# The first two projection blocks are begun without the adaLN shift, which is added later as a bias

## The chip, the cores and the metric

One core of one Trainium2 chip runs the whole program. The metric is device microseconds of one execution, on that core. TensorE is called PE here, the loads of its weights PEld, VectorE DVE, ScalarE ACT, GpSimd POOL, and SP is the queue engine that issues most DMAs.

## What is computed

One layer of a streaming encoder, for 1,024 prompt rows and 32 sample rows of width 1,024 (together 1,056 columns when transposed). Only the beginning matters here:

```python
mod = jax.nn.silu(c) @ w_ada + b_ada                # c: one row for the prompt, one for the sample
sh1, sc1, gt1, sh2, sc2, gt2 = jnp.split(mod[:, None, :], 6, axis=-1)
h = rmsnorm(x, g_mix) * (1 + sc1) + sh1
u = h @ w_in                                        # w_in: 1024 x 5640
qa, ka, va, qm, km, vm, om, ip, fp, ga, gm = jnp.split(u, _split_points(), axis=-1)
...
merged = (jax.nn.sigmoid(ga) * (ya @ w_br_att) + jax.nn.sigmoid(gm) * (ym @ w_br_mlstm))
x = x + gt1 * (merged @ w_out)
```

Band attention (`qa`, `ka`, `va`), an mLSTM (`qm` to `fp`), the merge by the gate columns `ga` and `gm`, and a SwiGLU FFN follow. Everything is float32, and a matmul of float32 precision is made from three passes over operands split in a high and a low part.

## The kernel before, in words

Activations stand transposed, 128 channels by 1,056 columns, in eight such rows of tiles (index `j` or `k`, 0 to 7). The 1,056 columns are taken in three tiles of 352, the constant `TILES`; the third tile holds the last 320 prompt columns and the 32 sample columns. `h` is kept as eight tiles `[128, 2, 1056]`, where part 0 is the value rounded to the matmul's type (written by ACT) and part 1 the remainder (written by DVE). A weight block is 128 columns of `w_in`, split the same way. One block times one tile is 8 x 3 = 24 matmuls of 128x352 (`unit`), a whole block 72.

Every engine runs its instructions in the order in which the program writes them (`manual_schedule`); DMAs on SP's queue also start in order, and each waits for the earlier DMA that used the same one of eight semaphores. The SBUF pool `slots` has 16 buffers of 128x2x1056, which hold in turn the rows of x, x transposed, the adaLN columns, normalised x and h; the pool `wsp` has four buffers for split weights; PSUM's pool `mm` has three buffers of 128x512.

The front runs like this:

- SP loads the small parameters, x, the adaLN weight's first 2,048 columns (`load_ada`, shift and scale together, eight loads of 128x2048), and weight blocks. PE transposes x (line 300), ACT copies it out of PSUM.
- `first_ada` makes shift and scale from these columns. PE takes ten of sixteen 128-column groups (line 337); DVE multiplies and adds six for both vectors of c (lines 341 and 343), and PE sums those over the partitions (line 351).
- `first_mod` adds the bias of adaLN and makes `sh1` and `s1` (lines 361, 364). `scaled_x` (line 373) makes x times scale and 1/rms, and `first_h` adds shift: ACT the high part (line 380), DVE the low part (line 384).
- x transposed is stored to DRAM as `xres` (eight stores, line 1438), for the residual sum much later.
- `first_units` (line 460) runs k_block(0) and v_block(0), the attention's first key and value blocks, together: per `k` three tiles of both blocks, as soon as h's tile `k` is there. Six PSUM tiles hold the sums.

Then `segs` lists segments of blocks. The first has k, v and q of the first two heads, the following ones the other blocks while attention and the mLSTM run beside them in steps that a counter releases (`side`). Sixteen blocks are gates; `gate_block` copies each tile out of PSUM and stores it to DRAM (`g_d`). Eight of the gate blocks stand in the last segment, beside the second half of the mLSTM.

Of the kernel before, what the change touches and what calls it, by code (L numbers as in the profile page):

```python
# [12 lines left out]
ALU = mybir.AluOpType  # L13
# [126 lines left out]
def hybrid_stream_step(  # L140
# [75 lines left out]
    sp.dma_start(prow[R_C:R_C + 8], c_prompt.rearrange("o (r c) -> (o r) c", c=P))  # L216
    sp.dma_start(prow[R_C + 8:R_C + 16], c_sample.rearrange("o (r c) -> (o r) c", c=P))
    xtok = []
    def param_loads():
        sp.dma_start(prow[R_ADA:R_ADA + 48], b_ada.rearrange("o (r c) -> (o r) c", c=P))  # L220
        sp.dma_start(prow[R_GMIX:R_GMIX + 8], g_mix.rearrange("o (r c) -> (o r) c", c=P))
        sp.dma_start(prow[R_GFFN:R_GFFN + 8], g_ffn.rearrange("o (r c) -> (o r) c", c=P))
        sp.dma_start(prow[R_GAIN:R_GAIN + 4], mh_gain.rearrange("o (r c) -> (o r) c", c=P))
        sp.dma_start(prow[R_CW:R_CW + 32], conv_w.rearrange("o j (r c) -> (o j r) c", c=P))
        sp.dma_start(prow[R_CB:R_CB + 8], conv_b.rearrange("o (r c) -> (o r) c", c=P))

    for i in range(KD):
        if i % 2 == 0:
            xt = slot([P, 2, D])
            xtok += [xt[:, 0], xt[:, 1]]  # L230
        sp.dma_start(xtok[i], xp[i * P:(i + 1) * P])
        if i == 3:
            param_loads()
# [47 lines left out]
    was = []  # L281

    def load_ada(n):
        while len(was) < n:
            wa = slot([P, 2048])
            sp.dma_start(wa, w_ada[len(was) * P:(len(was) + 1) * P, 0:2048])
            was.append(wa)

    load_ada(5)
# [34 lines left out]
    psA = [ps_s(), ps_t()]  # L324
    NV = 6
    acv = [tmpt((P, NV * P)) for _ in range(2)]

    def first_ada():
        load_ada(6)
        W.load(2)  # L330
        load_ada(KD)
        W.load(3)
        for k in range(KD):
            c = csil[:, k].unsqueeze(1).to_broadcast([P, DH, 2])
            for b in (*range(8, 16), *range(NV, 8)):
                out = psA[b // 8][:, (b % 8) * P:(b % 8 + 1) * P]
                pe.matmul(out.rearrange("p (r c) -> p r c", c=2), was[k][:, b * P:(b + 1) * P], c,
                          start=(k == 0 and b in (NV, 8, 12)), stop=(k == KD - 1), skip_group_check=True)
            for c in range(2):
                if k == 0:  # L340
                    dve.tensor_scalar(acv[c], was[k][:, :NV * P], csil[:, k, c:c + 1], None, op0=ALU.mult)
                else:
                    dve.scalar_tensor_tensor(acv[c], was[k][:, :NV * P], csil[:, k, c:c + 1], acv[c],
                                             op0=ALU.mult, op1=ALU.add)
            if k == 0:
                bcast_cols(RB, rstd, [P] * 8 + [TS], 0)
            if k == 3:
                W.advance()
        for b in range(NV):
            for c in range(2):  # L350
                pe.matmul(psA[0][:, b * P + c:b * P + c + 1], acv[c][:, b * P:(b + 1) * P], ones[:, 0:1],
                          start=(b + c == 0), stop=True, skip_group_check=True)
# [4 lines left out]
    def first_mod(i, a=0, b=KD):  # L357
        x = (sh1, s1)[i][:, :, a:b]
        p3 = psA[i].rearrange("p (b r) -> p r b", r=P)
        o = R_ADA + 8 * i  # L360
        dve.tensor_tensor(x, p3[:, 0:2, a:b], cols[:, o + a:o + b].unsqueeze(1).to_broadcast([P, 2, b - a]),
                          op=ALU.add)
        if i:
            dve.scalar_tensor_tensor(s1, s1, 1.0, bc2(cols[:, R_GMIX:R_GMIX + 8]), op0=ALU.add, op1=ALU.mult)

    hs = []

    def scaled_x(j):
# [3 lines left out]
        for c, a, b in col_segments(0, T):  # L372
            dve.scalar_tensor_tensor(xns[j][:, a:b], xTs[j][:, a:b], s1[:, c, j:j + 1], RB[:, a:b],
                                     op0=ALU.mult, op1=ALU.mult)

    def first_h(j):

        h = slot([P, 2, T], F32R)
        for c, a, b in col_segments(0, T):
            act.activation(h[:, 0, a:b], xns[j][:, a:b], AF.Identity, bias=sh1[:, c, j:j + 1])  # L380
        if j + 1 < KD:
            scaled_x(j + 1)
        for c, a, b in col_segments(0, T):
            dve.scalar_tensor_tensor(h[:, 1, a:b], xns[j][:, a:b], sh1[:, c, j:j + 1], f(h[:, 0, a:b]),
                                     op0=ALU.add, op1=ALU.subtract)
        hs.append(h)
# [10 lines left out]
    def weight(parts, nk, uses=3, home=None):  # L397
# [10 lines left out]
        def split(raw):  # L408
# [5 lines left out]
            for i, t in enumerate(wt):  # L414
                n = min(4, nk - 4 * i)
                split_to(t[:, :, :n], raw[:, 4 * i:4 * i + n], pool if (W.done or home is slots) and not hm_n[1] else dve)
# [21 lines left out]
    first = {}  # L438

    def first_units(ws):  # L440

        wts = [W.use(w) for w in ws]
        S, PT = ps_s(), ps_t()
        pts = [[mmt() for _ in TILES], [S[:, :512], S[:, 512:], PT[:, :512]]]
        for k in range(KD):
# [4 lines left out]
            if k == 6:  # L450
                W.advance()
# [1727 lines left out]
```

## Time and profile before

| | us |
|---|---|
| median of 3 runs (1636.94 to 1639.3) | 1638.59 |
| the profiled execution | 1638.16 |
| span of its profile | 1636.4 |
| PE busy | 1588.6 |
| DVE busy | 1123.2 |
| ACT busy | 782.3 |
| POOL busy | 535.7 |

The profile is one execution. In a row of a timeline the first two numbers are start and duration in us, xN is a count of instructions merged, and the bracket is the engine's idle time before the row with what ended it. In a group the numbers behind the bar are busy us, the mean in ns of one, and idle us before. A stretch A:B shows busy us of each engine, the share of full clock that PE was granted, the share of the DMA engines and GB/s. A name such as "s<-mm" says what is written and what is read.

### The profile page before, as it was taken

What the parts mean: (1) busy time and instruction counts of PE and PEld (TensorE: products, weight loads), DVE (VectorE), ACT (ScalarE), POOL (GpSimd) and SP (SyncE); (2) the same over time, 40 slices, a digit from 0 to 9 for tenths busy, and PEclk for the clock granted to TensorE, in tenths of its full rate; (3) what the DMA queues carried; (4) which work ended last, traced back from release to release, by engine and by line L of the source; (5) the groups of instructions that cost most, each with busy time, mean ns of one, the idle gap of its engine ahead of it and who ended that gap; (6) DMA issues with size and microseconds to landing.
All of it is one profiled execution on the core that took longest, in us unless ns stands there. A gap on an engine that the chain in (4) does not pass through costs nothing.

```text
span 1636.4 us, 27518 instructions
## 1 busy us (share of the span) xinstructions
PE 1588.6 (97%) x10324; PEld 1567.1 (96%) x10324; DVE 1123.2 (69%) x2100; ACT 782.3 (48%) x1735; POOL 535.7 (33%) x537
## 2 busy tenths in 40 slices
PE   6989999999999999999999998999999999999997
PEld 6989999999999999999999988999999999999997
DVE  6756564546776745446655688889888886898654
ACT  3455454543555544443434545454544444554443
POOL 1234333433432311000012146556565652233101
PEclk9999999999999999999999999999999999999999
DMA  9732323232232232574453311223223227426454
GB/s 338 249 107 75 106 81 106 68 120 79 76 94 79 59 100 69 118 275 160 129 151 107 98 53 40 92 66 103 80 67 103 66 82 246 132 78 236 133 158 126
DMA packets 210327, 192.45 MB, mean 118 GB/s; under 512 B 10571, under 2 KB 180531, under 8 KB 209171
## 3 DMA queue, kind: packets, MB, share of 16 engines
q1 hardware_dynamic: 205554, 187.88, 36.9%
q10 hardware_dynamic: 4640, 2.82, 0.6%
q8 instruction: 81, 1.33, 0.3%
q14 instruction: 52, 0.42, 0.1%
HBM read 152.19 MB, written 41.63 MB: 118 GB/s over the span
## 4 chain that ended last, share of the span: by engine, by line
PE 82%; DVE 6%; ACT 3%; issue 2%; DMA 1%; POOL 0%; ACTq 0%; POOLq 0%; DVEq 0%
PE mm L428 36%; PE psb L1727 27%; PE psb L2131 5%; PE psb L1974 3%; PE mm L826 2%; PE psV L725 2%; PE psS L667 1%; PE psT L694 1%; DVE s L1577 1%; DVE wsp L395 1%; DVE sl L1564 1%; DVE st L681 1%; PE psV L1060 1%; ACT st L682 1%; PE psT L1062 1%
## 5 line engine op out<-in xcount | busy, mean ns | idle before, releaser
L428 PE MATMUL mm<-s,wsp 128*128 128x352 f32 x4104 | 690.4, 324 | 5.7 <-DVE t L1658 1.9
L428 PEld LDWEIGHTS mm<-s,wsp 128*128 128x128 f32 x4104 | 656.8, 188 | 8.9 <-DVE stg L518 2.2
L1727 PE MATMUL psb<-s,wsp 128*128 128x352 f32 x2544 | 421.0, 323 | 8.9 <-DVE wsp L395 2.8
L1727 PEld LDWEIGHTS psb<-s,wsp 128*128 128x128 f32 x2544 | 411.1, 189 | 10.8 <-issue 5.3
L395 DVE TENSOR_TENSOR wsp<-wraw,wsp 128x512 fp32r<-128x512 f32 (+1 forms) x284 | 245.4, 882 | 126.0 <-ACT wsp L394 124.1
L394 ACT ACTIVATE wsp<-wraw 128x512 fp32r<-128x512 f32 x340 | 201.6, 617 | 144.9 <-PE psb L1727 81.9
L687 POOL TENSOR_SCALAR st<-st,mx 128x640 f32<-128x640 f32 (+5 forms) x72 | 55.6, 773 | 191.5 <-DVE mx L686 177.2
L1142 DVE SCALAR_TENSOR_TENSOR t<-wa,cmix,t 128x512 f32<-128x512 f32 x112 | 89.2, 801 | 13.7 <-DMA wa<-in_w_ada_dram 13.4
L395 POOL TENSOR_TENSOR wsp<-wraw,wsp 128x512 fp32r<-128x512 f32 x56 | 75.6, 1371 | 51.3 <-ACT wsp L394 50.8
L2131 PE MATMUL psb<-s,wsp 128*128 128x352 f32 x528 | 86.7, 324 | 0.0
L2131 PEld LDWEIGHTS psb<-s,wsp 128*128 128x128 f32 x528 | 84.7, 188 | 0.0
L682 ACT ACTIVATE st<-st,mx 128x640 f32<-128x640 f32 (+5 forms) x72 | 47.9, 665 | 72.6 <-DVE mx L681 72.5
L1727 PE MATMUL psb<-x,wsp 128*128 128x352 f32 x432 | 80.1, 324 | 2.5 <-DVE x L1577 2.5
L681 DVE CUSTOM_DVE_ANT_0 st<-psS,bias 128x640 f32<-128x640 f32 (+5 forms) x72 | 44.4, 617 | 54.6 <-PE psS L667 42.2
L1677 POOL TENSOR_TENSOR t<-t,sl 128x352 f32<-128x352 f32 x18 | 17.4, 967 | 185.3 <-ACT sl L1675 185.3
L1727 PEld LDWEIGHTS psb<-x,wsp 128*128 128x128 f32 x432 | 71.4, 189 | 2.9 <-DVE x L1577 2.9
L701 ACT ACTIVATE pT<-psT 128x640 fp32r<-128x640 f32 (+3 forms) x80 | 38.6, 493 | 68.8 <-PE psT L694 49.0
L1765 DVE TENSOR_TENSOR t<-t,psb 128x352 f32<-128x352 f32 x120 | 60.4, 511 | 5.1 <-PE psb L1727 4.9
L1362 POOL TENSOR_TENSOR wraw<-wraw 128x512 f32<-128x512 f32 x25 | 37.1, 1483 | 74.7 <-DVE wsp L395 73.8
L706 DVE TENSOR_TENSOR pT<-psT,pT 128x640 fp32r<-128x640 f32 (+3 forms) x80 | 44.0, 558 | 20.4 <-ACT pT L701 20.3
L1362 POOL TENSOR_TENSOR wraw<-wraw,raw 128x512 f32<-128x512 f32 x33 | 55.8, 1703 | 0.9
L826 PE MATMUL mm<-s,s 128*128 128x264 f32 (+3 forms) x432 | 54.8, 283 | 0.0
(352 smaller groups left out, 2337.5 us busy)
## 6 DMA issues: line engine op xcount, KB each, us to landing
wraw<-in_w_in_dram SPq DMA_DIRECT2D x40, 512.0 KB, 4.1
wraw<-in_w_gate_up_dram SPq DMA_DIRECT2D x33, 512.0 KB, 3.9
wa<-in_w_ada_dram SPq DMA_DIRECT2D x64, 256.0 KB, 3.0
wraw<-in_w_down_dram SPq DMA_DIRECT2D x32, 512.0 KB, 3.6
a_d<-t SPq DMA_DIRECT2D x22, 528.0 KB, 2.9
g_d<-t SPq DMA_DIRECT2D x16, 528.0 KB, 2.7
x<-xres SPq DMA_DIRECT2D x16, 528.0 KB, 5.1
t<-g_d SPq DMA_DIRECT2D x16, 528.0 KB, 5.3
```

Source lines behind the costliest of these rows:

```text
L394: act.activation(dst[:, 0], src, AF.Copy)
L395: eng.tensor_tensor(dst[:, 1], src, f(dst[:, 0]), op=ALU.subtract)
L428: pe.matmul(pt[:, :hi - lo], wt[(w0 + k) // 4][:, a, (w0 + k) % 4], xt[k][:, b, lo:hi], start=(k == 0 and q == 0), stop=(k == n - 1 and q ...
L681: dve.tensor_tensor_reduce(so, sv, bi, -1.0, 3.0e38, ALU.add, ALU.min, mx[:n, 1:2])
L682: act.activation(st[:n, :w], st[:n, :w], AF.Exp, bias=mx[:n, 1:2], scale=-1.0, accum_out=mx[:n, 2:3])
L687: pool.tensor_scalar(st[:n, :w], st[:n, :w], mx[:n, 3:4], 1.0, op0=ALU.mult, op1=ALU.mult)
L826: pe.matmul(pt[:n, :wd], hs[k][:, a, i * P:i * P + n], whl[b][:, k, :wd], start=(k == 0 and q == 0), stop=(k == KD - 1 and q == 2))
L1142: dve.scalar_tensor_tensor(ac[:, c], wa, cmix[:, c, k:k + 1], ac[:, c], op0=ALU.mult, op1=ALU.add)
L1362: pool.tensor_tensor(a(dst), a(x), a(y), op=op)
L1727: pe.matmul(acc, wt[:, a, k], x[k][:, b], start=(start and not onto and k == 0 and q == 0), stop=(stop and k == 3 and q == 2), skip_group_ ...
L1765: dve.tensor_tensor(c, c, y, op=ALU.add if sign > 0 else ALU.subtract)
L2131: pe.matmul(acc, wt[(k - k0) // 4][:, u, (k - k0) % 4], piece_of[k, 2][:, v], start=(k == 0 and q == 0), stop=(k == NF - 1 and q == 2))
```

## The change

The first two blocks are now gate columns: `ga`'s first two groups of 128 (`GA` to `GA + 256`). Their weights come in one load, `raw2`. h without the shift is enough to begin them on the first two tiles, since for prompt columns the shift adds to each output channel only a constant, W times `sh1`. That constant is made by 16 matmuls of two columns (`first_bias`) and added when the tile is copied out of PSUM. The third tile holds sample columns, whose shift is another, so it is not begun with the others.

- The small parameter loads go from SP's queue to ACT's.
- The adaLN weight is loaded as eight loads of scale columns (128x1024) and, behind them and behind `raw2`, eight of shift columns. All products with c are PE's; those for scale run ahead of the first blocks, those for shift between their `k` steps 0, 1 and 2. The part that DVE made is gone.
- `normed_x` makes x times 1/rms, `unshifted_h` h's first 704 columns with scale alone.
- When `sh1` is there, `shift_first` remakes normalised x with scale and shift: the third tile on DVE, the first two (704 columns) on POOL, and from them h's two parts by ACT and DVE. The first half of the 704-column parts is written after the first gate block's copies, the second half after the second's.
- The third tiles of the two gate blocks come then, and k, v and q after them with h complete. Two gates fewer are left for the last segment (six instead of eight), and the counter of `ada_rest`, the remaining adaLN work, goes from 495 to 472.

```diff
+    for k in range(KD):
+        if k % 2 == 0:
+            wa2 = slot([P, 2, D])
+        load_ada(1, k, wa2[:, k % 2])
+        if k == KD - 3:
+            sp.dma_start(raw2, w_in[:, GA:GA + 2 * P].rearrange("(k p) c -> p k c", p=P))
+    for k in range(KD):
+        load_ada(0, k, front.tile([P, D], F32, name=f"wsh{k}"))
...
+    def ada_products(i, k):
+        c = csil[:, k].unsqueeze(1).to_broadcast([P, DH, 2])
+        for b in range(KD):
+            out = psA[i][:, b * P:(b + 1) * P]
+            pe.matmul(out.rearrange("p (r c) -> p r c", c=2), was[i][k][:, b * P:(b + 1) * P], c,
+                      start=(k == 0 and b % 4 == 0), stop=(k == KD - 1), skip_group_check=True)
...
+        dve.tensor_tensor(xns[j], xTs[j], RB, op=ALU.mult)
+
+    def unshifted_h(j):
         h = slot([P, 2, T], F32R)
...
+        x, c, ts = xns[j], s1[:, 0, j:j + 1], slice(0, FIRST_T)
+        act.activation(h[:, 0, ts], x[:, ts], AF.Copy, scale=c)
+        dve.scalar_tensor_tensor(h[:, 1, ts], x[:, ts], c, f(h[:, 0, ts]), op0=ALU.mult, op1=ALU.subtract)
         hs.append(h)
+
+    def shifted_h(j, lo, hi, eng):
+        h, x = hs[j], xns[j]
+        for c, a, b in col_segments(lo, hi):
+            eng.tensor_scalar(x[:, a:b], x[:, a:b], s1[:, c, j:j + 1], sh1[:, c, j:j + 1],
+                              op0=ALU.mult, op1=ALU.add)
+        act.activation(h[:, 0, lo:hi], x[:, lo:hi], AF.Copy)
+        dve.tensor_tensor(h[:, 1, lo:hi], x[:, lo:hi], f(h[:, 0, lo:hi]), op=ALU.subtract)
...
+            for n in {0: (0, 1), 1: (2, 3, 4), 2: (5, 6, 7)}.get(k, ()):
+                ada_products(0, n)
+            if k == 2:
+                first_mod(0)
+                pb = ps_s()
+            if k == KD - 3:
+                for i in range(2):
+                    for n in range(KD):
+                        pe.matmul(pb[:, 2 * i:2 * i + 2], raw2[:, n, i * P:(i + 1) * P], sh1[:, :, n],
+                                  start=(i == 0 and n == 0), stop=(n == KD - 1), skip_group_check=True)
...
+    def shift_first():
+
+        lo, hi = TILES[2]
+        for j in range(KD):
+            if j == KD - 2:
+                dve.tensor_copy(bias1, first_bias.rearrange("p (i c) -> p i c", c=2)[:, :2, 0])
+            shifted_h(j, lo, hi, dve)
+        W.advance()
+        for a in range(0, KD, 4):
+            yield
+            for j in range(a, a + 4):
+                shifted_h(j, 0, FIRST_T, pool)
+        yield
...
         def run():
             raw = tmpt()
-            for lo, hi in TILES:
+            done = first.get(id(w), ())
+            for (lo, hi), pt in zip(TILES, done):
+                act.activation(raw[:, lo:hi], pt, AF.Identity, bias=bias1[:, nth:nth + 1])
+            if done:
+                next(shifts)
+            for lo, hi in TILES[len(done):]:
                 pt = unit(w, 0, hs, lo, hi)
                 act.activation(raw[:, lo:hi], pt, AF.Copy)
             sp.dma_start(g_d[2 * j + g], raw)
```

Three places show how the order moves. In each row stand the line, the operation, what it writes and reads, the size written and the semaphores it waits for; DMAHW0 to 7 are those of the DMAs.

SP's queue around the stores of x transposed (`s_123` and `s_124` are its first two pairs; `wsh` are shift columns, `wraw` weight blocks). Before:

```order
L286 DMA s_317<-in_w_ada_dram 128x2048 [waits DMAHW2_49]
L404 DMA wraw_319<-in_w_in_dram 128x8x128 [waits DMAHW3_49]
L404 DMA wraw_396<-in_w_in_dram 128x8x128 [waits DMAHW6_49,DMAHW4_49,DVE_49]
L404 DMA wraw_398<-in_w_in_dram 128x8x128 [waits DMAHW7_49,DMAHW5_49,DVE_49]
L1438 DMA xres<-s_123 128x1056 x2
L1438 DMA xres<-s_124 128x1056 [waits DMAHW0_49]
```

And now:

```order
L278 DMA wsh_156<-in_w_ada_dram 128x1024 [waits DMAHW0_49]
L278 DMA wsh_158<-in_w_ada_dram 128x1024 [waits DMAHW1_49]
L386 DMA wraw_643<-in_w_in_dram 128x8x128 [waits DMAHW2_49]
L386 DMA wraw_645<-in_w_in_dram 128x8x128 [waits DMAHW3_49]
L1468 DMA xres<-s_123 128x1056 [waits DMAHW4_49,Activation_49]
L1468 DMA xres<-s_123 128x1056 [waits DMAHW5_49,Activation_49]
L1468 DMA xres<-s_124 128x1056 [waits DMAHW6_49,Activation_49]
```

The stores keep their place behind the adaLN columns, with two weight blocks in front of them in the second part of the queue; the first two use semaphores 4 and 5.

DVE where scale and shift are made (`s_285` and `s_306` are scale, `sh` shift, `s_462` and the like x scaled or normalised, the other outputs h). Before:

```order
L361 TENSOR_TENSOR s_285<-psT_281,cols 128x16 [waits PE_49]
L364 SCALAR_TENSOR_TENSOR s_285<-s_285,cols 128x16 [waits DVE_49]
L373 SCALAR_TENSOR_TENSOR s_462<-s_123,s_285,t_279 128x1024 [waits DVE_49]
L373 SCALAR_TENSOR_TENSOR s_462<-s_123,s_285,t_279 128x32
L361 TENSOR_TENSOR sh_284<-psS_280,cols 128x2x2 [waits PE_49]
```

Now, from the fifth h on:

```order
L359 SCALAR_TENSOR_TENSOR s_425<-s_406,s_306,s_425 128x704 [waits DMAHW2_49,DMAHW1_49,Activation_49]
L359 SCALAR_TENSOR_TENSOR s_428<-s_406,s_306,s_428 128x704 [waits DMAHW4_49,DMAHW3_49,Activation_49]
L359 SCALAR_TENSOR_TENSOR s_431<-s_419,s_306,s_431 128x704 [waits DMAHW6_49,DMAHW5_49,Activation_49]
L359 SCALAR_TENSOR_TENSOR s_434<-s_419,s_306,s_434 128x704 [waits DMAHW5_49,DMAHW4_49,Activation_49]
L342 TENSOR_TENSOR sh_305<-psT_303,cols 128x16 [waits PE_49]
L365 TENSOR_SCALAR s_391<-s_391,s_306,sh_305 128x320 [waits DVE_49]
L365 TENSOR_SCALAR s_391<-s_391,s_306,sh_305 128x32
L368 TENSOR_TENSOR s_403<-s_391,s_403 128x352 [waits Activation_49]
```

The shift moved from ahead of the first h to behind the low part of the last one (`s_434`, which takes the buffer of `s_123` and waits for semaphores 4 and 5).

ACT behind the last h, and PE behind the first pass (`mm_437` is the first gate column's first tile, `mm_712` its third). Before, on ACT:

```order
L380 ACTIVATE s_665<-s_610,sh_284 128x1024 [waits DMAHW6_49,DMAHW7_49,DVE_49,Activation_49]
L380 ACTIVATE s_665<-s_610,sh_284 128x32 [waits DVE_49]
L497 ACTIVATE s_688<-mm_476 64x352 [waits PE_49,Activation_49]
L497 ACTIVATE s_688<-mm_476 64x352
L497 ACTIVATE s_688<-mm_477 64x352 [waits PE_49]
```

Now, on ACT:

```order
L367 ACTIVATE s_425<-s_406 128x352 [waits DVE_49]
L367 ACTIVATE s_428<-s_406 128x352 [waits DVE_49]
L367 ACTIVATE s_431<-s_419 128x352 [waits DVE_49]
L367 ACTIVATE s_434<-s_419 128x352 [waits DVE_49]
L376 ACTIVATE s_688<-wraw_643 128x512 [waits DMAHW1_49,DMAHW2_49,DMAHW0_49,PE_49]
L376 ACTIVATE s_688<-wraw_643 128x512
L622 ACTIVATE t_697<-mm_437,bias_311 128x352 [waits PE_49]
L622 ACTIVATE t_697<-mm_438,bias_311 128x352 [waits PE_49]
L367 ACTIVATE s_403<-s_391 128x704 [waits Pool_49]
```

And on PE:

```order
L441 MATMUL mm_438<-s_434,wsp_308 128x352 x3
L441 MATMUL mm_439<-s_434,wsp_310 128x352 x3
L441 MATMUL psV_440<-s_434,wsp_310 128x352 x3
L410 MATMUL mm_712<-s_403,wsp_307 128x352 [waits Activation_49]
L410 MATMUL mm_712<-s_403,wsp_307 128x352
L410 MATMUL mm_712<-s_403,wsp_307 128x352 [waits DVE_49]
L410 MATMUL mm_712<-s_408,wsp_307 128x352 x2
```

Between the last h and the first copy out of PSUM, ACT now has the third-tile parts of all eight h and the split of k_block's weights; PE's first matmul of the third tile waits for ACT and its later rows, of `s_408` and so on, no longer do.

## What is predicted

> **What bounds the kernel now.** I read the page's shares first, then the busy time by stretches of 10 us, then each engine's own rows over the first 80 us, and last the prices of single instructions.
>
> ```profile
> span 1636.4 us, 27518 instructions
> PE 1588.6 (97%) x10324; PEld 1567.1 (96%) x10324; DVE 1123.2 (69%) x2100; ACT 782.3 (48%) x1735; POOL 535.7 (33%) x537
> PE 82%; DVE 6%; ACT 3%; issue 2%; DMA 1%; POOL 0%; ACTq 0%; POOLq 0%; DVEq 0%
> ```
>
> PE is busy for 97% of the span and makes 82% of the chain that ended last. So a change at the front is worth the time by which PE reaches the same point of its work earlier or later, if nothing behind it gives that back.
>
> ```profile
> 0.00:10.00 10.00, 2.16 (x7) 1.31 (x8) 4.29 (x7) 1.53 (x2) 1.11 (x12) 1.00 0.70 242
> 10.00:20.00 10.00, 5.81 (x35) 5.04 (x34) 5.09 (x9) 4.50 (x9) 0.00 (x0) 0.94 0.95 319
> 20.00:30.00 10.00, 9.70 (x74) 8.89 (x73) 7.53 (x12) 6.78 (x20) 3.27 (x6) 0.88 1.02 414
> 30.00:40.00 10.00, 10.00 (x90) 10.00 (x90) 6.78 (x10) 2.73 (x6) 0.00 (x0) 1.00 1.05 373
> 40.00:50.00 10.00, 8.56 (x78) 8.48 (x76) 7.95 (x13) 1.32 (x3) 0.00 (x0) 0.98 1.10 353
> 50.00:60.00 10.00, 10.00 (x54) 10.00 (x55) 10.00 (x16) 5.38 (x9) 0.00 (x0) 0.85 0.84 335
> ```
>
> The columns are PE, weight loads, DVE, ACT and POOL busy, then granted clock, DMA share and GB/s. The DMA engines are full from 10 to 50 us. The second view is PE's row order, with two rows of DVE and one of ACT behind it.
>
> ```profile
> 19.08 1.33 PE L300 MATMUL mm<-ident,s 128*128 128x128 f32 x5 [1.75 <-DMA s<-in_x_prompt_dram]
> 29.97 2.05 PE L337 MATMUL psT<-csil,s 128*128 128x128 f32 x16
> 32.31 1.95 PE L337 MATMUL psT<-csil,s 128*128 128x128 f32 x16
> 45.71 2.73 PE L351 MATMUL psS<-ones,t 128*128 128x1 f32 x24
> 49.88 2.13 PE L460 MATMUL mm<-s,wsp 128*128 128x352 f32 x6 [1.44 <-ACT s L380]
> 74.61 2.66 PE L428 MATMUL mm<-s,s 128*128 128x352 f32 x15
> 37.03 7.68 DVE L343 SCALAR_TENSOR_TENSOR t<-s,csil,t 128x768 f32<-128x768 f32 x8
> 45.46 0.17 DVE L361 TENSOR_TENSOR s<-psT,cols 128x16 f32<-128x16 f32 x1 [0.76 <-PE psT L337]
> 48.68 2.61 ACT L380 ACTIVATE s<-s,sh 128x1024 fp32r<-128x1024 f32 x4 [12.37 <-DVE sh L361]
> ```
>
> The last x rows land at 19.08. The adaLN products keep PE to 45.71 and DVE (7.68 us in one piece) to 44.7; scale is ready at 45.5, shift at 48.6, and the first product of a projection starts at 49.88. The two first blocks (144 matmuls of 128x352) are through at 74.61. That is the mark: when has the changed kernel done 144 such matmuls (its two gate columns, three tiles each)?
>
> **The change, part by part.** Prices first. A projection matmul comes from a stretch with nothing else in it: 20.00 us for 127, 0.1575 us each. An adaLN matmul is (32.31 - 29.97) / 20 = 0.117 us (16 shown and 4 of another group between).
>
> ```profile
> 740.00:760.00 20.00, 20.00 (x127) 20.00 (x126) 1.00 0.54 181
> L394 ACT ACTIVATE s<-x 128x352 fp32r<-128x352 f32 x68 | 28.9, 484 | 0.0
> L394 ACT ACTIVATE s<-t 128x1056 fp32r<-128x1056 f32 x4 | 4.3, 1086 | 5.3 <-DMA t<-ya_d 5.3
> L1577 DVE TENSOR_TENSOR s<-x,s x8: 507/510/511, 992.3 to 997.0; 128x352 fp32r<-128x352 f32 x8
> L1140 DVE TENSOR_SCALAR t<-wa,cmix 128x512 f32<-128x512 f32 x16 | 7.9, 491 | 0.2
> L2103 DVE SCALAR_TENSOR_TENSOR x<-s,amod,x 128x704 f32<-128x704 f32 x8 | 7.6, 945 | 0.0
> L687 POOL TENSOR_SCALAR st<-st,mx x72: 372/799/1320, 100.4 to 460.0; 128x640 f32<-128x640 f32 x32, 128x128 f32<-128x128 f32 x8, 128x256 f32<-128x256 f32 x8, 128x384 f32<-128x384 f32 x8
> ```
>
> *Start.* Before the first product now stand x (4.19 MB), the sample's x (0.13), the scale columns (4.19) and both gate columns (1.05): 9.56 MB instead of 13.8 (x, all of 2,048 adaLN columns, two blocks). By the stretches 9.75 MB had passed at 30 us. The small parameter loads leave SP's queue, where they stood between x's halves and held it at 242 and 319 GB/s; at 406 GB/s (row below) the 5.61 MB of the first 20 us cost 2.9 us less. The third load of x now waits for the landing of the first, so I count 2.0 of it. The last scale row lands near 28.7; its eight products 0.9, L342 and L344 0.35, ACT's 128x704 part 0.785 (between 484 and 1086 ns): PE starts at about 30.8, 19 us earlier. The DVE products of L341/L343 vanish.
>
> *First pass.* PE then has 96 projection matmuls (15.1), the 64 shift products that used to lie ahead (7.5), 16 bias matmuls at 2.73 / 24 = 0.11 (1.8), and about 1.7 at half clock as in the row at 50 us: done at 57. If that were all, 48 more (7.6) would end at 64.5, 10 us ahead of the mark.
>
> *Shift.* It is not all. On DVE the shift (L342) stands behind the low part of all eight h (L359), and the last h lives in the slot of the first x pair, so it waits until the first two stores of xres have landed. Those stand in SP's queue behind scale, gates, shift columns and two weight blocks: 15.88 MB up to the second.
>
> ```profile
> 4.00:6.00 2.00, 0.45 (x1) 0.18 (x1) 0.61 (x1) 0.00 (x0) 0.00 (x0) 1.00 1.02 406
> 42.00:44.00 2.00, 2.00 (x20) 2.00 (x19) 1.93 (x3) 0.00 (x0) 0.00 (x0) 1.00 1.22 296
> 56.00:58.00 2.00, 2.00 (x15) 2.00 (x14) 2.00 (x4) 0.79 (x2) 0.00 (x0) 1.00 0.64 240
> 42.60 9.59 SPq L1438 DMA_DIRECT2D xres<-s x8
> xres<-s SPq DMA_DIRECT2D x8, 528.0 KB, 7.2
> ```
>
> Before had moved 13.48 MB by 40 us and 15.88 by 46.8. From that go the 2.0 above and some 0.4 for two weight blocks in 512-byte pieces (296 GB/s) where five stood: 44.4. The last store was issued near 50.95 (8 issues up to 52.19), landed 7.2 later at 58.2, while the rate falls near 56.5: 1.7 from the last byte to the landing. So 46.1, then ACT 0.785, DVE's 128x704 0.945, L342 0.17 and three handovers of 0.04: **shift at 48.2**. PE has its products by 30.8 + 1.7 + 36 x 0.1575 + 7.5 = 45.7, so the stores decide.
>
> *Remaking.* The gate blocks' third tile needs a PSUM buffer that L622 frees, and on ACT L622 stands behind eight third-tile parts (L367) and the split of k_block's weights. Each of the eight is a round trip: DVE 320 + 32 columns 0.47 (from the 128x512 row, with overlap), ACT 0.484, DVE 0.51, two handovers, less 0.08 overlap: 1.46. Eight up to ACT's end 11.2, the bias copy 0.1, two splits 1.2, L622 0.46: 13.0 us after shift, if DVE is alone. It isn't: POOL begins its eight 128x704 remakes (0.80 for mostly 640 columns, so 0.87) at the same moment.
>
> ```profile
> 531.01 0.60 DVE L1091 TENSOR_SCALAR num<-num,dn 128x128 f32<-128x128 f32 x2
> 543.89 2.59 DVE L1091 TENSOR_SCALAR num<-num,dn 128x128 f32<-128x128 f32 x2 [0.87 <-POOL dn L1086]
> 543.83 2.53 POOL L395 TENSOR_TENSOR wsp<-wraw,wsp 128x512 fp32r<-128x512 f32 x2
> ```
>
> The same pair of DVE instructions takes 0.60 alone and 2.59 beside two of POOL's: each waits for one whole POOL instruction. The price of the eight lies between 0 (they fall into DVE's waits for ACT, 0.5 a trip) and 7.0 (none does). With turns taken in pairs as at 543.89, three trips meet them all and 1.9 of the 7.0 falls into waits: I take 5.1. **L622 frees the buffer at 48.2 + 13.0 + 5.1 = 66.3.** PE has idled since 57. The clock then is low, by the nearest rows:
>
> ```profile
> 48.00:50.00 2.00, 0.56 (x5) 0.48 (x5) 1.52 (x4) 1.32 (x3) 0.00 (x0) 0.91 1.04 418
> 50.00:52.00 2.00, 2.00 (x7) 2.00 (x8) 2.00 (x4) 1.29 (x3) 0.00 (x0) 0.50 1.01 410
> 52.00:54.00 2.00, 2.00 (x12) 2.00 (x11) 2.00 (x4) 1.34 (x2) 0.00 (x0) 0.74 1.03 416
> ```
>
> After a wait of 1.44 us the lost shares (0.18 + 1.00 + 0.52) make 1.7 us; I charge it again. 66.3 + 48 x 0.1575 + 1.7 = 75.6, against 74.61: **+1.0 us**.
>
> *The rest.* Behind the mark both kernels have the same blocks to do. The remaking of the first two tiles (L367/L368 on 704 columns) runs on ACT and DVE beside the 7.6 us of the gates' third tiles; its last low part comes near 77, k_block needs it 3.3 us after 75.6. The last segment has two gate blocks fewer beside the mLSTM; PE had no idle time there, and the segment before it runs the same steps over five blocks without any, so I take 0 (bounds 0 and 2). The parameter loads on ACT's queue end before its first evacuation: 0.
>
> The Trainium skill ("SBUF — State Buffer", Terms) says that DVE and GpSimd share a port pair under an exclusive lock, held for the full instruction, and that the loser fully blocks. The pair at 543.89 agrees. Charged that way throughout, with nothing under ACT's time, the eight would cost 7.0, shift's loop 20.0 and the sum +2.9 us; this is the second case below.
>
> **The rivals.** (1) POOL's work blocks DVE in full, 8 x 0.87 = 7.0: +2.9, 1641.5. For it: the 2.59. Against: DVE waits for ACT about 0.5 us a trip, which POOL can use. (2) POOL's instructions hide in those waits: the buffer is free at 61.2, PE's mark at 70.5, -4.1 us, 1634.5. For it: only eight such instructions against eight waits; against: 0.87 does not go into 0.5. (3) Slower: the front's DMA gains nothing over before, so the two stores end at 46.8 and shift comes at 50.6, 2.4 later; all behind shift is a chain, so +3.4, 1642.0. It decides from a shift 2.3 us later than mine. For it: the waits for earlier landings on SP's queue are still eight deep; against: at 10 to 20 us it held only 319 GB/s. (4) The change doesn't do what it says, and the first product stays near 45 us: then the first pass ends near 71 and the mark comes near 80, +6 or more. Against: its inputs are 9.56 MB.
>
> **How the numbers follow.** The profiled execution took 1638.16 for its 1636.4 span; the median of the runs is 1638.59, 0.43 more, and I add the changes to that. Likeliest is my sum, 1639.6 with a range of its own of 1637 to 1642: chance 0.40. Rival 1 has 0.13, rival 2 0.28, rival 3 0.15, rival 4 0.04. What a measurement here tells from no change is 0.2%, 3.3 us. Faster: rival 2 mostly, with a little of the sum's spread, 0.28. Slower: rivals 3 and 4, half of 1, a tenth or two of the sum's, 0.30. Same: 0.42. The range takes rival 2 and rival 3 in with 1 to 2 us of their own spread: 1633.5 to 1644.
>
> **What would show it.** PE's first L441 near 31; DVE's L342 of the shift near 48, with ACT's last L358 ended by a DMA; the eight L367 of 352 columns about 1.5 to 3 us apart, longer where POOL's L365 runs; PE idle before L410 of the first gate column, released by ACT L622, near 66; the end of 48 L410 near 75.6. I am wrong if that idle time is missing or under 3 us, if shift comes before 45, if POOL's eight leave DVE's times alone, or if the two kernels' distance changes between 75 us and the end.

## The result, and the profile after

The changed kernel takes 1653.17 us (median of 4 runs, 1652.0 to 1654.25) against 1638.94 (median of 4 runs, 1636.94 to 1640.92): ratio 1.0083, 95% interval 1.007 to 1.0096. It is 14.2 us slower. Its profiled execution took 1653.85, with a span of 1652.1.

The timeline of PE in the changed kernel (start, duration, line, what is written and read, shape, count, and the idle time before):

```profile
23.27 2.05 PE L332 MATMUL psS<-csil,s 128*128 128x128 f32 x16
27.37 12.77 PE L332 MATMUL psS<-csil,s 128*128 128x128 f32 x112
41.53 1.07 PE L441 MATMUL mm<-s,wsp 128*128 128x352 f32 x5 [1.39 <-ACT s L358]
43.58 3.73 PE L332 MATMUL psT<-csil,wsh 128*128 128x128 f32 x32
49.08 5.52 PE L332 MATMUL psT<-csil,wsh 128*128 128x128 f32 x48
56.37 5.52 PE L332 MATMUL psT<-csil,wsh 128*128 128x128 f32 x48
67.54 3.63 PE L451 MATMUL psS<-sh,raw 128*128 128x2 f32 x32
78.87 7.95 PE L410 MATMUL mm<-s,wsp 128*128 128x352 f32 x48 [2.20 <-ACT t L622]
86.66 8.53 PE L410 MATMUL mm<-s,s 128*128 128x352 f32 x52
```

The 144th projection matmul is done at 86.66 us, 12.05 later than before (74.61). The counts tell why. The program text has 64 products for scale and 64 for shift (`ada_products`), and 16 for the bias; the trace has 128, 128 and 32. Each matmul of two float32 operands is two PE instructions, 12.77 / 112 = 0.114 us each. Two stretches, of before and of after, each from the first adaLN product to the mark, show it in one row (PE busy, with its count, is the second number):

```profile
25.43:74.61 49.18, 47.74 (x348) 47.39 (x347) 40.53 (x56) 18.32 (x40) 5.10 (x3) 0.97 0.88 315
23.27:86.66 63.39, 59.80 (x452) 59.16 (x451) 36.68 (x56) 23.16 (x47) 9.72 (x9) 0.97 0.72 262
```

PE has 104 instructions more: 96 are DVE's old share of the products (six of sixteen column groups, eight rows, two each), 32 the bias, and the 24 column sums (L351) are gone. At 0.114 that is 11.9 us; PE's busy time grew by 12.06. It waits 2.1 us more (3.59 against 1.44) and began 2.16 earlier, which cancel. The earlier beginning is hardly the change's doing: in this profile of before the last x rows landed late, and runs 1 and 8, whose program is that of before up to there, begin these products at 23.12 and 23.66. PE was busy for 94 to 97% of both stretches, so its added work is the loss up to the mark; runs 1 and 9 test this.

Scale and shift both come when PE has made them, and not when a load or store lands. These are rows of DVE, ACT and POOL in the changed kernel:

```profile
40.18 0.17 DVE L342 TENSOR_TENSOR s<-psS,cols 128x16 f32<-128x16 f32 x1 [7.55 <-PE psS L332]
51.18 0.88 ACT L358 ACTIVATE s<-s,s 128x704 fp32r<-128x704 f32 x1 [1.15 <-DVE s L353]
61.93 0.17 DVE L342 TENSOR_TENSOR sh<-psT,cols 128x16 f32<-128x16 f32 x1 [7.38 <-PE psT L332]
62.29 9.44 POOL L365 TENSOR_SCALAR s<-s,s,sh 128x704 f32<-128x704 f32 x8 [38.75 <-DVE sh L342]
66.10 1.12 DVE L365 TENSOR_SCALAR s<-s,s,sh 128x320 f32<-128x320 f32 x2
67.25 0.50 ACT L367 ACTIVATE s<-s 128x352 fp32r<-128x352 f32 x1 [1.79 <-DVE s L365]
69.53 0.50 ACT L367 ACTIVATE s<-s 128x352 fp32r<-128x352 f32 x1 [1.78 <-DVE s L365]
72.78 0.65 DVE L365 TENSOR_SCALAR s<-s,s,sh 128x320 f32<-128x320 f32 x2
75.19 0.50 ACT L367 ACTIVATE s<-s 128x352 fp32r<-128x352 f32 x1 [1.23 <-DVE s L365]
76.84 0.50 ACT L367 ACTIVATE s<-s 128x352 fp32r<-128x352 f32 x1 [1.16 <-DVE s L365]
78.29 0.98 ACT L622 ACTIVATE t<-mm,bias 128x352 f32<-128x352 f32 x2
```

DVE idled 7.55 us for the scale products and 7.38 for the shift products. The last h (L358 at 51.18) was released by DVE, long before shift. Behind shift the remaking goes as the prediction has it: beside POOL a trip takes 69.53 - 67.25 = 2.28 us, without it 76.84 - 75.19 = 1.65, and the first L622 ends at 78.82, 16.9 after shift.

Behind the mark the distance grows from 12.05 to 14.3 by 987 us, and to 15.7 at the end of these two profiles. The first rows are of after at 120 us, where the half clock of the second stretch (column PEclk, the 0.50: PE runs at half its speed) follows a wait that before does not have; the last two are the same matmul group in before and after:

```profile
121.95 2.30 PE L410 MATMUL mm<-s,wsp 128*128 128x352 f32 x9 [2.00 <-DVE stg L543]
119.42:122.83 3.41, 1.42 (x9) 1.13 (x8) 0.77 (x3) 1.26 (x3) 0.96 (x2) 1.00 0.08 22
122.83:126.24 3.41, 3.41 (x14) 3.41 (x13) 0.00 (x0) 0.00 (x0) 0.00 (x0) 0.50 0.80 258
973.02 3.19 PE L428 MATMUL mm<-s,wsp 128*128 128x352 f32 x18 [1.69 <-ACT sl L1652]
987.33 3.99 PE L410 MATMUL mm<-s,wsp 128*128 128x352 f32 x23 [1.58 <-ACT sl L1684]
```

### The profile page after: what moved, and what is told of

Read it like the earlier page. It is cut to its first block, busy times and chain, and to the rows that moved or that the text cites. A ratio compares the mean times of both kernels' runs of the same rounds, so it can differ in the third digit from the quotient of the medians.

```text
span 1652.1 us, 27750 instructions
## 1 busy us (share of the span) xinstructions
PE 1602.0 (97%) x10428; PEld 1580.2 (96%) x10428; DVE 1122.1 (68%) x2098; ACT 788.1 (48%) x1743; POOL 551.2 (33%) x547
## 4 chain that ended last, share of the span: by engine, by line
PE 78%; DVE 7%; ACT 3%; issue 2%; DMA 1%; POOL 1%; ACTq 0%; POOLq 0%; DVEq 0%
PE mm L410 34%; PE psb L1759 25%; PE psb L2163 5%; PE mm L856 3%; PE psb L2006 3%; PE psV L755 2%; PE psS L697 1%; DVE wsp L377 1%; PE psT L724 1%; DVE s L377 1%; DVE s L1609 1%; DVE sl L1596 1%; PE psV L1090 1%; PE psT L1092 0%; PE psT L1087 0%
## 5 line engine op out<-in xcount | busy, mean ns | idle before, releaser
L410 PE MATMUL mm<-s,wsp 128*128 128x352 f32 x4152 | 702.1, 325 | 10.5 <-DVE stg L543 3.9
L410 PEld LDWEIGHTS mm<-s,wsp 128*128 128x128 f32 x4152 | 666.0, 189 | 15.1 <-DVE stg L543 4.8
L377 DVE TENSOR_TENSOR wsp<-wraw,wsp 128x512 fp32r<-128x512 f32 (+1 forms) x276 | 242.0, 894 | 104.3 <-ACT wsp L376 102.3
L377 POOL TENSOR_TENSOR wsp<-wraw,wsp 128x512 fp32r<-128x512 f32 x60 | 81.8, 1383 | 79.9 <-ACT wsp L376 77.8
L1395 POOL TENSOR_TENSOR wraw<-wraw,raw 128x512 f32<-128x512 f32 x33 | 55.7, 1701 | 0.9
```

What stands on the lines that cost most here:

```text
L377: eng.tensor_tensor(dst[:, 1], src, f(dst[:, 0]), op=ALU.subtract)
L410: pe.matmul(pt[:, :hi - lo], wt[(w0 + k) // 4][:, a, (w0 + k) % 4], xt[k][:, b, lo:hi], start=(k == 0 and q == 0), stop=(k == n - 1 and q ...
L1395: pool.tensor_tensor(a(dst), a(x), a(y), op=op)
```

## The experiments

Theory P: the loss is PE's added instructions. Rival L: loads and stores set scale and shift, and PE's products hide beside them. Rival R: the remaking behind shift, with the waits that it makes, is the loss. Each time is a median, taken beside the kernel before on the same chip; "+x" is the difference to its median there (1638.4 to 1639.9), and after itself stands at +14.2. An interval is about 2 us to either side, so two changed kernels are told apart from some 3 us on; the marks of the profiles are finer, but a profile is one execution. Three dots stand for lines of an edit that are left out. An edit moves the lines behind it by a few, so that a row can have L623 or L639 where the text says L622.

**1. The kernel before, with DVE's share given to PE** (no other part of the change).

```diff
-    NV = 6
-    acv = [tmpt((P, NV * P)) for _ in range(2)]
+    NV = 0
...
```

The DVE products and the column sums go with it.

> The kernel before, with VectorE's six blocks of shift columns (L343) given to TensorE, as the change does; nothing else is altered. Theory (front bound by TensorE's instruction count; a float32 product is two instructions of 0.114 us): 96 instructions more, 24 column sums fewer, 72 x 0.114 = +8.2 us, first L460 at about 58 instead of 49.9. Rival (front bound by its loads, 15.88 MB by 46.8 us; the products are hidden beside them): 0 to +2 us.

Measured 1647.91, +8.7 (ratio 1.0053, 1.004 to 1.0066). PE's timeline there:

```profile
55.72 1.24 PE L449 MATMUL mm<-s,wsp 128*128 128x352 f32 x6 [1.44 <-ACT s L369]
80.38 2.66 PE L417 MATMUL mm<-s,s 128*128 128x352 f32 x15
```

The theory's 8.2 lies inside the interval, the rival's 0 to 2 far outside. The first projection matmul comes at 55.7 instead of 58 because this execution's products begin 2.3 us earlier (23.12) than those in the profile of before (25.43), where PE waits for the last x rows until 19.08 instead of 17.29. So more than half of the loss belongs to one line of the change that the summary of it hardly mentions.

**2. The changed kernel, with four of scale's eight groups on DVE.**

```diff
-        for b in range(KD):
+        for b in range(4 * i, KD):
...
+        for c in range(2):
...
+                dve.scalar_tensor_tensor(acv[c], was[1][k][:, :NV * P], csil[:, k, c:c + 1], acv[c],
+                                         op0=ALU.mult, op1=ALU.add)
...
```

> The changed kernel, with four of the eight blocks of scale columns on VectorE (which idles from 20 to 28 and from 33 to 40 us). Theory: 64 TensorE instructions fewer, 16 column sums more, 48 x 0.114 = 5.5 us less; first projection matmul near 36 instead of 41.5, mark near 81. Rival (the loads or the remaking behind shift set the mark): 0 to -2 us.

Measured 1654.87, +15.6: nothing gained, a miss.

```profile
33.37 1.84 PE L473 MATMUL psS<-ones,t 128*128 128x1 f32 x16
38.06 1.83 PE L443 MATMUL mm<-s,wsp 128*128 128x352 f32 x5 [2.85 <-ACT s L360]
32.04 4.76 DVE L355 TENSOR_TENSOR s<-s,t 128x1056 f32<-128x1056 f32 x4
77.43 7.95 PE L412 MATMUL mm<-s,wsp 128*128 128x352 f32 x48 [2.19 <-ACT t L634]
```

PE has its products 4.9 us earlier (35.2 against 40.1), but DVE normalises x behind its own products, until 36.8, and the first matmul gains 3.5. Then a half clock behind the narrow sums and around the wait (0.50 in the two 3.41 us stretches from 35.8 on) takes more; shift comes at 60.5, L622 ends 16.9 after it as before, and the mark is at 85.22, 1.4 earlier. The rest lies behind the mark. Work taken from PE alone turns into waiting for the chain behind shift.

**3. Shift's products earlier in PE's order.**

```diff
-            for n in {0: (0, 1), 1: (2, 3, 4), 2: (5, 6, 7)}.get(k, ()):
+            for n in {0: (0, 1, 2, 3, 4), 1: (5, 6, 7)}.get(k, ()):
...
```

> The changed kernel, with five of the eight rows of shift products written ahead of the second k step (two before) and the rest behind it. TensorE's work is the same. Theory: shift comes 2 to 4 us earlier than 61.9, the wait of 2.2 us before the gates' third tile goes and with it the half clock behind it (1.7): -3.9 us, the end of the first pass stays at 76.7. Rival (shift's columns land too late, or L622 is held by something else than shift): 0, with TensorE waiting before L332 or still before L410.

Measured 1651.72, +12.5. Shift comes at 59.58, L622 ends at 76.60, 17.0 after it, and the wait before the third tile is gone:

```profile
77.70 7.84 PE L410 MATMUL mm<-s,wsp 128*128 128x352 f32 x48
```

But the mark is 85.38, 1.3 earlier and not 3.9: the half clock does not go, it lasts longer (70.0 to 76.8). So it was not that wait which halved it; run 5 takes this up.

**4. The sample rows' staging tile in a buffer of its own**, for the wait at 120 us. DVE's copy of v's sample rows (L518 in before, L543 in after) waits in both kernels for the landing of a store:

```profile
86.60 0.28 DVE L518 COPY stg<-mm 32x128 f32<-32x128 f32 x1 [2.66 <-DMA out_dram<-stg]
121.62 0.28 DVE L543 COPY stg<-mm 32x128 f32<-32x128 f32 x1 [6.45 <-DMA out_dram<-stg]
```

In before PE still has matmuls up to 88.57 and does not feel it. In after the store is that of v's prompt rows: it is issued at 115.83, just behind the loads of the two caches (114.59 and 115.22), and lands 5.6 us later, while PE's matmuls end at 119.95. Whether those loads make the landing late is not shown.

```diff
-        stg = ap_.tile([P, 4, P], F32, tag="stg", name=nm("stg"), bufs=2)
+        stg = ap_.tile([P, 1, P], F32, tag="stgs", name=nm("stgs"), bufs=1)
         dve.tensor_copy(stg[:TS, 0], pt[:TS, :P])
```

> The changed kernel, with the sample rows' staging tile in a buffer of its own, so that v_block's copy L543 no longer waits for the store of v_block's prompt rows, which the two cache loads were moved ahead of. Theory: the wait of 2.0 us at 120 us and the half clock behind it (1.7) go: -3.7 us. Rival (another wait takes its place): 0 to -1.

Measured 1650.09, +10.8: 3.4 us of the 14.2.

```profile
115.31 8.91 PE L410 MATMUL mm<-s,wsp 128*128 128x352 f32 x54 [0.49 <-ACT stg L549]
```

54 matmuls now run where 24 and a wait stood. The difference to after is at the edge of what these runs can tell, but the mechanism stands in the rows.

**5. The bias product 128 columns wide instead of 2**, as many instructions.

```diff
-    pe.matmul(pb[:, 2 * i:2 * i + 2], raw2[:, n, i * P:(i + 1) * P], sh1[:, :, n],
+    pe.matmul(pb[:, i * P:(i + 1) * P].rearrange("p (r c) -> p r c", c=2),
+              raw2[:, n, i * P:(i + 1) * P], sh1[:, :, n].unsqueeze(1).to_broadcast([P, DH, 2]),
...
```

> The changed kernel; the 32 bias instructions (L451) write 128 columns (shift broadcast 64 times) instead of 2, as the adaLN products do. Their number is the same. Theory (a stretch of 3.4 us in which TensorE works on 2 columns at a time counts as idle for its clock, and the next 3.41 us run at half speed): no half clock at 71.6 us, the first pass ends 1.7 us earlier, at 75; but L622 stands at 78.9 behind shift, so that the wait before the third tile grows from 2.2 to 3.9 and the time stays within 0.5 us, or loses 1.7 if that wait in its turn halves the clock. Rival (the clock drops for another reason): half clock stays at 71.6.

Measured 1656.85, +18.4. The clock in after, and here (share of the clock behind the POOL column):

```profile
68.22:71.63 3.41, 3.41 (x31) 3.41 (x31) 2.85 (x6) 0.50 (x1) 3.41 (x3) 1.00 0.46 175
71.63:75.04 3.41, 3.41 (x13) 3.41 (x13) 2.28 (x8) 1.00 (x2) 0.10 (x1) 0.50 0.03 9
```

```profile
68.93:72.34 3.41, 3.41 (x26) 3.41 (x26) 2.81 (x6) 0.50 (x1) 1.69 (x2) 1.00 0.39 144
77.75 9.50 PE L410 MATMUL mm<-s,wsp 128*128 128x352 f32 x48 [3.72 <-ACT t L623]
79.17:82.58 3.41, 3.41 (x13) 3.41 (x12) 2.98 (x4) 1.70 (x3) 0.00 (x0) 0.50 0.57 154
```

As the theory says, the half clock at 71.6 goes, the first pass ends at 74.0, and PE waits 3.72 us for L622, after which the clock is halved there instead. The other profiles bear the theory out: all five with the narrow bias (after, 2, 3, 4 and 9) have a halved stretch that begins in it or right behind it, and of the five with the wide one (5, 6, 7, 10 and 11) none has one before PE has waited 1.7 us or more. The mark, 87.09, is 0.4 later. The total is 4.2 over after, more than the 1.7 expected at worst; behind the mark this execution has five half-speed stretches, where after has two, up to 3 x 1.7 us, enough to account for it.

**6. Three edits together:** 3, 4 and 5.

> The changed kernel with three edits together: shift's products earlier, the sample stage in its own buffer, and bias written 128 columns wide. Theory: no wait and no half clock from 40 us up to the mark, no wait at 119 us: mark near 82 instead of 86.66, total -4.7 - 3.7 = -8.4, about 1645, still 5 to 6 us over the kernel before, the price of TensorE's added instructions. Rival (the waits make the whole loss): as fast as the kernel before.

Measured 1649.09, +10.7. The wait at 119 us is gone, but not the one before the third tile:

```profile
76.61 9.51 PE L410 MATMUL mm<-s,wsp 128*128 128x352 f32 x48 [1.76 <-ACT t L623]
```

The first pass ends at 74.86 and L622 at 76.56, 16.9 after shift (59.66); the half clock follows the wait. Mark 85.96 instead of 82. The rival fails too: with fewer waits the kernel is still 10.7 over before.

**7. Those three, scale's four groups on DVE, and gate 0's copies (L622) ahead of the last third-tile part.**

> The kernel of the run ahead of it, with four blocks of scale columns on VectorE as well (x's first normalised part ahead of its last rows, the others behind scale; column sums 64 wide) and gate 0's L622 ahead of the last third-tile part. Theory: 48 instructions fewer, the first projection matmul near 36.6, mark near 78, total 1653 - 8.4 - 4.5 = about 1640.5, level with the kernel before or 1 to 3 us over it. Rival (VectorE's work again comes late and takes it back): as the run ahead of it, 1645.

Measured 1651.64, +13.2; the mark 84.00 instead of 78. The first projection matmul is at 36.56, as expected, but DVE now normalises each x just ahead of ACT's part of it and waits for ACT in between, so that shift is read at 59.39, 2.9 us after PE has made it, and L622 ends at 73.60.

```profile
73.65 9.51 PE L412 MATMUL mm<-s,wsp 128*128 128x352 f32 x48 [1.91 <-ACT t L639]
84.00 0.42 PE L412 MATMUL mm<-s,s 128*128 128x352 f32 x1 [0.84 <-ACT s L378]
```

The clock is also halved for a stretch at 36.60 and for one at 74.15, 1.7 us each, and PE waits 0.84 us for the split of the next weights. Of the 4.6 us by which the first matmul is earlier than in run 6 (41.18), 2.0 are left at the mark. Behind it this execution has four halved stretches and run 6's two, which is 3.4 us.

**8. The kernel before with the column sums 64 wide.**

```diff
-                pe.matmul(psA[0][:, b * P + c:b * P + c + 1], acv[c][:, b * P:(b + 1) * P], ones[:, 0:1],
+                out = psA[0][:, b * P:(b + 1) * P].rearrange("p (r c) -> p r c", c=2)[:, :, c]
+                pe.matmul(out, acv[c][:, b * P:(b + 1) * P], ones[:, 0:1].to_broadcast([P, DH]),
```

> The kernel before; the 24 column sums behind adaLN (L351) write 64 columns instead of 1. Theory (narrow matmuls count as idle for the clock): the half clock at 49.6 to 53.0 us goes, -1.7 us, the end of the first two blocks at 72.9. Rival (the wait of 1.44 us behind them halves the clock): 0.

Measured 1638.81, +0.4 (ratio 1.0003, 0.9994 to 1.0013). The stretch behind the sums, first in before and then here:

```profile
49.62:53.03 3.41, 3.15 (x11) 3.15 (x12) 3.41 (x8) 2.04 (x5) 0.00 (x0) 0.50 1.03 414
```

```profile
47.86:51.27 3.41, 1.97 (x11) 1.70 (x12) 3.41 (x6) 2.39 (x4) 0.00 (x0) 1.00 1.03 414
918.25:921.66 3.41, 3.41 (x30) 3.41 (x30) 3.41 (x6) 2.38 (x5) 0.00 (x0) 1.00 0.43 135
921.66:925.07 3.41, 3.41 (x14) 3.41 (x13) 0.60 (x8) 1.75 (x2) 1.65 (x1) 0.50 0.96 282
```

The half clock went, and the mark came 1.1 us earlier (73.51). But so did the first projection matmul (48.83 against 49.88): from there to the mark both take 24.7 us, DVE being full there. So the half clock at 50 us cost before nothing at its mark, and the time is the same. Later stretches are halved instead, such as the one at 921.66, behind 24 one-column sums at 918 to 920 that before has too, without that loss. (The profiled execution took 1642.15, more than the median.)

**9. The changed kernel without half of shift's products.**

```diff
-            for n in {0: (0, 1), 1: (2, 3, 4), 2: (5, 6, 7)}.get(k, ()):
+            for n in {0: (0, 1), 1: (2, 3)}.get(k, ()):
...
```

> The changed kernel without the shift products of rows 4 to 7 (their weights are still loaded, shift is left unfinished): 64 TensorE instructions fewer, nothing else. Theory: shift comes when VectorE has its eight low parts, 54.6 instead of 61.9 us, the first pass ends 7.3 us earlier, and so does the mark: 79.4; total -7.3 (within 1.7 either way by half clocks). Rival (loads, stores or the remaking alone set the mark): shift earlier, the mark within 2 us of 86.7.

This kernel leaves shift unfinished. Measured 1647.45, +7.6, so 6.6 less than after.

```profile
54.18 0.17 DVE L342 TENSOR_TENSOR sh<-psT,cols 128x16 f32<-128x16 f32 x1
71.11 7.95 PE L410 MATMUL mm<-s,wsp 128*128 128x352 f32 x48 [0.22 <-ACT t L622]
```

64 instructions x 0.114 = 7.3; the mark is 78.91, 7.75 earlier (0.3 of it because the first matmul came at 41.25). Shift is read as soon as DVE has its low parts, L622 ends 16.9 behind it. This settles P against L: with every load and store in place, removing PE's products moves shift, the first pass and the mark at once. The remaking is all there too, so R is not the whole of the loss either.

**10. Run 6 with POOL's eight L365 held back** until DVE's loop is nearly done: they read the copy `sh1b` instead of `sh1`.

```diff
+            if j == KD - 2:
+                dve.tensor_copy(sh1b, sh1)
...
```

> The kernel of e6 (shift early, sample stage of its own, bias 128 wide), with POOL's eight L365 held back: they read a copy of shift that VectorE makes ahead of its last third-tile part. Theory (VectorE's L365 is blocked by POOL's): eight even trips of 1.68 us, L622 at shift + 15.2 instead of + 16.9, as the first pass ends; the wait of 1.76 us and the half clock behind it go: -3.5 against e6, mark near 82.5. Rival (POOL's instructions cost VectorE nothing on its path): trips and L622 as in e6. A third way: POOL's late parts hold the first k_block up and give 1 to 3 us back.

Measured 1647.06, +7.2. That is 3.5 less than run 6 by the differences to before, and 2.0 by the times as they are; the two were taken on different chips.

```profile
61.12 0.65 DVE L365 TENSOR_SCALAR s<-s,s,sh 128x320 f32<-128x320 f32 x2
70.59 0.16 DVE L486 COPY bias<-psS 128x2 f32<-128x2 f32 x1 [1.09 <-PE psS L452]
75.75 7.96 PE L410 MATMUL mm<-s,wsp 128*128 128x352 f32 x48 [1.35 <-ACT t L626]
```

DVE's pair takes 0.65 in every trip up to the copy of shift, where it took 1.12 beside POOL, and trips are 1.66 apart. The faster loop then runs into the bias, which PE has not made yet (1.09), so L622 ends at 75.70, 16.5 behind shift; the wait is 1.35, no half clock follows, and the mark is 83.54. Behind it 52 matmuls follow without a wait, so POOL's late parts held nothing up.

**11. Run 10 with scale's four groups on DVE**, x normalised two ahead.

> The kernel of e10 with four blocks of scale columns on VectorE (as in e7, but x's parts are normalised two ahead, so that VectorE does not wait for ScalarE at each). Theory: first projection matmul near 36.6, shift near 56.5, first pass to 71.7 and L622 at the same time: mark near 79.3, total 1642 to 1643, still 3 to 4 us over the kernel before. Rival (VectorE is late again): as e10 or slower.

Measured 1647.59, +7.7. The mark is 80.39, 3.15 earlier than in run 10, and near the 79.3 expected; the total is the same. Behind the mark this execution has four half-speed stretches, run 10's two, which is 3.4 us. No version here beats the kernel before.

**12. The kernel before with the small loads on ACT's queue**, one part of the change alone.

> The kernel before with one part of the change alone: the eight small parameter loads on ACT's queue instead of SP's. Theory: as in the changed kernel (first adaLN product at 23.3 instead of 25.4 us), TensorE's unbroken stretch up to 46 us begins 2 us earlier and ends 2 us earlier: -2 us, at the edge of what can be told. Rival (the last adaLN rows' loads set the end of that stretch): -0 to -1.

Measured 1640.91, +2.0 (ratio 1.001, 1.0001 to 1.0019). The products begin at 22.5 and end 1.9 earlier than in the profile of before. Against runs 1 and 8 (23.12 and 23.66), which have these loads on SP, the beginning gains only 0.7 to 1.2, and PE then waits for rows of the adaLN weight, as the rival says:

```profile
36.42 2.05 PE L330 MATMUL psT<-csil,s 128*128 128x128 f32 x16 [0.21 <-DMA s<-in_w_ada_dram]
```

The clock is halved from 46.5 to 53.3, the mark gains 0.9, and the total nothing.

## Why the prediction was wrong, point by point

It forecast +1.0 with a range of -5 to +5; +14.2 was measured. The step that failed is the count of PE's work in **Start** and **First pass**. "Its eight products 0.9" and "the 64 shift products (7.5), 16 bias matmuls (1.8)" took the calls in the program text, and the price of one instruction in the trace; PE had to run 128, 128 and 32 instructions. The trace of before had the answer, in the prediction's own rows: 16 + 4 instructions a row for ten column groups, so two for each. And "the DVE products vanish" was half the truth: the groups had moved to PE, which the same timeline showed busy without a gap from 23 to 48 us.

- *First L441 near 31:* 41.53. The scale products alone take 128 x 0.114 = 14.6 us from 23.3 on, with 2.2 of other matmuls between. Bytes did not decide it: the queue had delivered in time (DVE waited for PE, not for a load). It was later than forecast all the same: at 233, 375 and 391 GB/s after had moved 9.99 MB by 30 us, against 9.75 in before, a gain of 0.6 us where 2.0 was taken (the 2.9 ahead of it does not follow from its terms: 5.61 MB at 406 GB/s take 13.8 of the 20 us). In run 7 DVE waits for the last scale row until 31.49, not 28.7. So this part of rival 3 was nearly right, and hidden behind PE.
- *Shift near 48, after the stores:* (its terms add up to 48.1) 61.93, after PE. The stores' landing did not end ACT's last L358; run 9 with half the products read shift at 54.18 with the same stores, as soon as DVE had its low parts.
- *Remaking, 18.1 from shift to L622:* 16.9 in after and in runs 2, 5, 6 and 9, 17.0 in run 3. The mechanism was right. A trip alone is 1.66 and not 1.46, and POOL's blocking costs 2.3 in all (four trips 0.5 to 0.6 longer), where 5.1 was taken from a range of 0 to 7.0. The Trainium skill ("SBUF — State Buffer", Terms) speaks of a lock held for the full instruction; the rows agree that DVE loses time beside POOL, 1.12 against 0.65 a pair. That is 0.47, less than POOL's 0.92 to 1.45; whether a pair waits for the rest of a POOL instruction that has begun, the rows do not tell.
- *PE idles from 57 to 66.3:* 2.20, from 76.67 to 78.87, and so under the 3 us that the prediction gave as a sign of being wrong. The late shift was expected to leave PE without work; PE was itself late by as much. With the true counts, after's start of the products (23.3), its other matmuls between (2.2) and its wait behind them (1.4), and the prediction's other prices, the first L441 comes at 23.3 + 14.6 + 2.2 + 1.4 = 41.5, the first pass ends at 41.5 + 15.1 + 14.6 + 3.6 + 1.7 = 76.5 (76.67 measured), shift comes at 41.5 + 36 x 0.1575 + 14.6 = 61.8, L622 at 61.8 + 18.1 = 79.9, and the mark near 87.5: +13.
- *Half clock of 1.7 after the wait:* there is one, but at 71.6, behind the bias (run 5). The one in before from which the price was taken cost nothing at the mark (run 8).
- *The rest, 0 to 2:* 2.3 by 987 us, to which the wait and half clock at 120 us belong (2.0 and 1.7; run 4), and another 1.4 later, in code that is the same.
- *Rivals:* the fourth (first product near 45, mark near 80, "+6 or more", chance 0.04) was the nearest in its signs, but named no cause beyond a change that does not do what it says. None had PE as the bound of the front.

Why single repairs moved so little: two chains end within 2.2 us of each other at the mark, PE's own work (76.67) and shift plus 16.9 (78.8). Run 5 moves mainly the first, and run 3 only the second; run 2 brings both forward by only 1.4 us. Only runs 7 and 9 to 11 moved both by over 2 us.

Not settled: why before and after differ by 1.4 us more in the last 650 us; the profiles have half-speed stretches in other places there, and one profile of each can't tell how often each falls where.

## What to carry to other kernels

Count an engine's added work in instructions of the trace, never in calls of the program: take the number and the price from the same row, and check the number against a row where the call count is known. Before costing an earlier start by what has been loaded, look whether the engine that starts is idle; where a stretch reads 10.00 busy of 10.00, moved work is added work. When two chains end close together, judge a repair by the later of both.

## What the runs showed of the hardware

Half clock comes in stretches of 3.41 us (or multiples), on a fixed grid within an execution: after's begin at 71.63, 122.83 and 1034.19, which are 15.0 and 267.0 stretches apart. Which stretch is halved depends on the one before it. Behind the first 12 us, with PE waiting 1.85 us or more of it, the next was nearly always halved (in after, that behind 2.00 at 119.42 was, that behind 1.89 at 1440.38 was not); between 1.68 and 1.84 sometimes (that behind 1.68 in run 4 at 129.11 was, that behind 1.79 in after at 75.05 was not). And narrow matmuls count like waiting: a stretch mostly of 128x2 matmuls, without a gap, was followed by 0.50 (68.22), the same 32 instructions 128 wide were not (run 5). As they cost 0.113 us each narrow and 0.117 wide (3.63 / 32 and 3.74 / 32), width is nearly free there. From which width on they count as work is not shown: in run 7 a stretch with 1.39 us of waiting and sixteen sums 64 wide was followed by half clock (36.60). The Trainium skill ("TensorE: Matmul & The Clock Gate", Part 1) states a free-running window of 3413 ns, which these rows bear out, and puts the half clock after an idle window; here a window half idle was enough. Since the grid lies elsewhere in each execution, a wait of about 2 us costs 1.7 more in one and nothing in the next (run 6's of 1.76 lay within one stretch and was followed by half clock, after's of 2.20 fell on two and was not): the profiles here have 1 to 8 halved stretches ahead of 1,628 us, and edits worth 1 to 2 us (8, 12) disappear in that.
